# An attention stretch whose vector work follows the matmuls by hand, with z's norm on GpSimd

## The chip, the cores and the metric

The kernel runs on one core of a Trainium2 chip. A core has five engines with instruction streams of their own: TensorE (PE: matmuls and transposes into PSUM banks), VectorE (DVE), ScalarE (ACT), GpSimd (POOL) and SyncE (SP, which issues DMA transfers). Each executes its stream strictly in order, and an instruction that reads another engine's result waits on a semaphore; everything behind it on its engine waits too. The metric is the device time of one execution in microseconds; several executions are timed and the median is given.

## The reference, cut to what matters

One block of a streaming encoder on 512 tokens of width 1024, in f32: attention in two head groups, a gated feed-forward layer with a short convolution, and a gated embedding. The change touches the first group and the preparation of the second:

```python
h = rms_norm(x, attn_norm_g)
z = h @ W_in      # MLA q-latent 256 | kv-latent 128 | rope key 32 | diff q 512 | diff k 512 | diff v 512
# 8 MLA heads: q and k of 96 (64 + 32 with rope), v of 64, both normed per head
logits = q k^T * 96**-0.5;  masked;  probs = softmax(logits);  o = probs v
# 4 differential heads, each with two halves of 64:
q = rms_norm(dq.reshape(..., 4, 2, 64), q_g);  k = rms_norm(dk.reshape(..., 4, 2, 64), k_g)
logits = q k^T / 8 + bias[bucket(key - query)]
attn = softmax(first half) - lam * softmax(second half);  o = attn v
...
x += concat(o_mla, o_diff) @ W_out;  x += conv_ffn(x);  x += gated embedding
```

A query block of 128 sees only the keys up to its own block, since the mask is causal over chunks of 64.

## The kernel before, in words

All matmuls run in f32r; each operand is split into a high half (a cast on ScalarE, `hi`) and a low half (a subtraction on VectorE, `lo`), and a product is three matmuls (`mm3`, lines 157 to 159). Tokens lie in four blocks t = 0 to 3 of 128.

The MLA stretch (lines 771 to 832) is a loop over 16 steps i = 4 hp + t: pairs of heads hp = 0 to 3, query blocks t. A step makes, for the pair's two heads c:
- `mla_logits`: the logits of block t + 1 (TensorE), their negated maxima and the scaling of these (VectorE), and the exponentials with their sums (ScalarE);
- `mla_norm`: reciprocals of block t's sums and the scaling of its probabilities `pm` (VectorE);
- `mla_T`: transposes of block t's probabilities (TensorE, `pTm`) and copies of them to SBUF (`pt`, by VectorE or ScalarE in turn);
- `mla_pv`: the product with the values for the block before (TensorE, `mo`).
At t = 2 and t = 3 `mla_q` and `mla_k` transpose the next pair's queries and keys (`qT`, `kT`), and `split` makes their high and low halves `st`. Logits use three PSUM banks ("lg"), transposes two ("tp"): a transpose can start only when the tile before the last one has been read from its bank.

To keep TensorE busy between these, `pump(n)` inserts n *fill units* of the projection z = h W_in for the differential heads (`zd_units`): six matmuls each. The column blocks are c = 0 (queries), 1 (keys), 2 (values); c = 0 is done before the loop, c = 1 needs its units up to step 6, c = 2 the rest. `FILL_MLA = (1, 2, 2, 2)` is the number of units at t = 0 to 3. Weights of z come in four pieces per block (d0x, d1x, d2x), loaded by SP into three rotating raw buffers, then cast and subtracted.

`zd_out` scales a finished z block on ScalarE, squares it, and reduces the squares to `ssd` on VectorE. `zd_norm(c)` then makes the reciprocal roots `rd` of all 32 columns (4 blocks x 8 half-heads) by a Newton iteration on VectorE (`rms_v`), and scales the four blocks. `rms` is the other way to such a root that the kernel has: one VectorE operation and one GpSimd power (line 165).

`bias_strip` (step 3) builds the relative bias: GpSimd writes a row of 640 values, and issues three DMA transfers, each waiting for the one before (to memory, spread over 128 rows in memory, and back skewed), then a MEMSET on the tile that came back. Its row `vb` uses the buffer of an earlier z square.

What sets the order: TensorE's order is that of the code throughout. For VectorE, ScalarE and GpSimd a region with the same rule is open from the start of the kernel to step 2 (`region.__exit__`); after it a scheduler places their instructions, with a few held behind a named instruction (`tc.issue_after`), until a later region in the feed-forward part.

## Time and profile before

| | us |
|---|---|
| median of 3 runs | 652.36 (650.77 to 652.65) |
| profiled execution | 651.15 |
| its span, first to last instruction | 649.4 |
| TensorE busy in the span | 634.6 (98%) |
| VectorE, ScalarE, GpSimd busy | 489.2, 361.4, 57.5 |
| MLA stretch | about 66 to 165 of the span |

The granted clock of TensorE was 0.999 of full speed. Times in the rows below are microseconds from the span's start. A row of a timeline gives start, duration, engine, line and operation, output and inputs, shape, how many instructions are merged, and in brackets how long the engine was idle just before and which engine's instruction ended that. Buffer numbers are left out of the names: `st<-kT` stands for the split of any head's keys, `pTm` for any transposed probabilities.

### The profile page before, as it was taken

The numbers are of one execution on the slowest core, as the hardware profiler recorded it, in microseconds if no ns is written. First come the engines' busy times: TensorE is split into PE (matmuls) and PEld (weight loads), VectorE is DVE, ScalarE is ACT, GpSimd is POOL, SyncE is SP. The second block draws the span as 40 slices with busy tenths as digits, with TensorE's granted clock in tenths as the row PEclk, the third lists the DMA queues.
The fourth block names the chain that finished last, engine by engine and source line by source line (L and its number), as shares of the span: only waits on it lengthen the run. The fifth ranks groups of instructions, "written<-read, shape, count | busy, mean of one in ns | idle before, by whom it ended". The sixth has DMA issues, their size and how long they took to land.

```text
span 649.4 us, 10234 instructions
## 1 busy us (share of the span) xinstructions
PE 634.6 (98%) x3900; PEld 556.3 (86%) x3900; DVE 489.2 (75%) x898; ACT 361.4 (56%) x629; POOL 57.5 (9%) x92
## 2 busy tenths in 40 slices
PE   9999899899999999999999999999999999999997
PEld 9988677778788887889999999999999999988886
DVE  6889678668788776888886767676767677769844
ACT  7897557357567455656554645554554645547211
POOL 1510050000000121000100000000001100000000
PEclk9999999999999999999999999999999999999999
DMA  8351226033120337536675646465646463541121
GB/s 307 93 163 53 77 75 202 2 131 129 35 64 2 137 108 242 148 95 180 170 198 144 186 114 179 116 186 127 190 114 179 114 179 115 179 129 47 44 89 50
DMA packets 29913, 82.64 MB, mean 127 GB/s; under 512 B 3100, under 2 KB 4124, under 8 KB 29736
## 3 DMA queue, kind: packets, MB, share of 16 engines
q1 hardware_dynamic: 23816, 69.17, 32.0%
q0 software_dynamic: 5616, 12.33, 11.1%
q8 instruction: 31, 0.51, 0.3%
q10 hardware_dynamic: 432, 0.49, 0.2%
q14 instruction: 18, 0.15, 0.1%
HBM read 77.77 MB, written 5.52 MB: 128 GB/s over the span
## 4 chain that ended last, share of the span: by engine, by line
PE 84%; DVE 10%; ACT 4%; issue 1%; DMA 1%; ACTq 0%
PE dn L157 6%; PE dn L158 6%; PE dn L159 6%; PE gx L159 4%; PE gx L158 4%; PE gx L157 4%; PE g L157 3%; PE g L158 3%; PE g L159 3%; PE o L157 3%; PE o L159 2%; PE pg L159 2%; PE pg L158 2%; PE o L158 2%; PE pg L157 2%; PE zd L157 2%
## 5 line engine op out<-in xcount | busy, mean ns | idle before, releaser
L903 DVE TENSOR_TENSOR wSl<-rS,wSh 128x1024 fp32r<-128x1024 f32 x21 | 25.7, 1224 | 43.9 <-ACT wSh L899 43.7
L157 PE MATMUL dn<-ah,hi_dn 128*128 128x512 f32 x144 | 56.2, 391 | 0.0
L158 PE MATMUL dn<-al,hi_dn 128*128 128x512 f32 x144 | 56.2, 391 | 0.0
L159 PE MATMUL dn<-ah,lo_dn 128*128 128x512 f32 x144 | 56.0, 389 | 0.0
L1020 POOL DMA_DIRECT2D rS<-in_w_gu x19 | 22.7, 1195 | 250.6 <-DVE cv L1188 128.9
L899 ACT CAST wSh<-rS 128x1024 fp32r<-128x1024 f32 x21 | 22.1, 1052 | 36.1 <-PE gy L158 35.8
L157 PE MATMUL zd<-hi_d,xh 128*128 128x512 f32 x96 | 39.2, 409 | 0.0
L158 PE MATMUL zd<-lo_d,xh 128*128 128x512 f32 x96 | 37.8, 394 | 0.9 <-DVE lo_d L305 0.9
L669 DVE TENSOR_TENSOR x<-x,dn 128x512 f32<-128x512 f32 x44 | 29.9, 680 | 6.1 <-PE dn L159 6.1
L903 DVE TENSOR_TENSOR wTl<-rA,wTh 128x1024 fp32r<-128x1024 f32 x19 | 23.3, 1225 | 14.5 <-ACT wTh L899 14.0
L159 PEld LDWEIGHTS dn<-ah,lo_dn 128*128 128x128 f32 x144 | 27.0, 188 | 5.8
L157 PEld LDWEIGHTS dn<-ah,hi_dn 128*128 128x128 f32 x144 | 27.1, 188 | 5.1
L158 PEld LDWEIGHTS dn<-al,hi_dn 128*128 128x128 f32 x144 | 27.1, 188 | 5.0
L903 DVE TENSOR_TENSOR wAl<-rA,wAh 128x1024 fp32r<-128x1024 f32 x21 | 25.6, 1217 | 2.2 <-ACT wAh L899 2.2
L1191 ACT ACTIVATE cv<-cv 128x512 f32<-128x512 f32 x22 | 13.9, 631 | 23.9 <-DVE cv L1188 23.8
L899 ACT CAST wAh<-rA 128x1024 fp32r<-128x1024 f32 x21 | 22.1, 1053 | 8.9 <-DMA rA<-in_w_gu 8.6
L157 PE MATMUL g<-b2h,wAh 128*128 128x256 f32 (+1 forms) x88 | 26.4, 300 | 0.6 <-ACT g L1144 0.6
L157 PE MATMUL o<-yh,hi_o 128*128 128x512 f32 x64 | 26.9, 420 | 0.0
L718 ACT ACTIVATE pmd<-pmd,nmd 128x128 f32<-128x128 f32 (+3 forms) x32 | 17.9, 561 | 15.9 <-DVE nmd L717 15.9
L590 ACT ACTIVATE pm<-ml,sums,rq 128x128 f32<-128x128 f32 (+3 forms) x32 | 19.5, 616 | 12.6 <-DVE sums L583 7.5
L158 PE MATMUL g<-b2l,wAh 128*128 128x256 f32 (+1 forms) x88 | 26.3, 299 | 0.0
L159 PE MATMUL g<-b2h,wAl 128*128 128x256 f32 (+1 forms) x88 | 26.2, 297 | 0.0
(480 smaller groups left out, 2198.9 us busy)
## 6 DMA issues: line engine op xcount, KB each, us to landing
rA<-in_w_gu SPq DMA_DIRECT2D x22, 512.0 KB, 3.8
rS<-in_w_gu SPq DMA_DIRECT2D x22, 512.0 KB, 3.6
rS<-in_w_gu POOLq DMA_DIRECT2D x19, 512.0 KB, 6.0
raw_dn<-in_w_down SPq DMA_DIRECT2D x18, 512.0 KB, 5.9
raw_d<-in_w_d SPq DMA_DIRECT2D x12, 512.0 KB, 3.4
r<-in_w_gu SPq DMA_DIRECT2D x19, 256.0 KB, 5.8
raw_o<-in_w_out SPq DMA_DIRECT2D x8, 512.0 KB, 3.9
rS_pg<-in_w_pg SPq DMA_DIRECT2D x6, 512.0 KB, 4.0
```

The lines of the kernel that those rows point to most:

```text
L157: TE.matmul(ps, xh, wh, start=first and i == 0, stop=False, skip_group_check=again)
L158: TE.matmul(ps, xh, wl, start=False, stop=False, skip_group_check=again)
L159: TE.matmul(ps, xl, wh, start=False, stop=last and i == n - 1, skip_group_check=again)
L590: S.activation(pm[c], ps[c], AF.Exp, bias=nm[:, c:c + 1], scale=r[:, c:c + 1], accum_out=ssum[:, c:c + 1])
L669: V.tensor_tensor(xb(b), xb(b), ps, op=ALU.add)
L718: S.activation(pm[:, :n], pm[:, :n], AF.Exp, bias=nm, scale=-1.0, accum_out=s0 if m == 0 else s1)
L899: S.copy(h_, src)
L903: V.tensor_tensor(l_, src, _f32(h_), op=ALU.subtract)
L1020: nc.gpsimd.dma_start(sums[f].rearrange("p (i c) -> p i c", i=2), a["w_gu"][f][:, :2048].rearrange("p (i c) -> p i c", i=2)[:, :, :512], a ...
L1191: S.activation(cv, cv, AF.Silu)
```

## The change

The order of VectorE, ScalarE and GpSimd is that of the code through the whole MLA stretch: the region is closed in step 15 and not in step 2, and the `issue_after` holds in between are gone. The code is put in this order:
- `mla_norm` of a block comes ahead of the next block's logits (for t > 0), and the exponentials are a function of their own (`mla_exp`), at t = 2 one behind `mla_q` and one behind `mla_k`;
- `zd_norm` is split in two: `zd_root(c)` makes the roots by `rms`, so with a GpSimd power on 128x32, and `zd_scale(c, t)` scales one block. `rms_v` is no longer used for them;
- a table `extra` gives each step its share of the roots, of the scalings and of the casts and subtractions of the weights d2x; a second table, `late`, gives the first splits for the output product, behind the fill units of steps 13 and 14;
- `FILL_MLA` is (2, 1, 2, 2): one fill unit goes from t = 1 to t = 0.

```diff
-FILL_MLA = (1, 2, 2, 2)
+FILL_MLA = (2, 1, 2, 2)
...
-    def zd_norm(c):
-        rms_v(rd[:, c].rearrange("p t m -> p (t m)"), ssd[:, c].rearrange("p t m -> p (t m)"), 8 * NT, 64)
-        for t in range(NT):
-            zv = zd[c][t].rearrange("p (m d) -> p m d", d=64)
-            V.tensor_tensor(zv, zv, rd[:, c, t, :].unsqueeze(2).broadcast_to([P, 8, 64]), op=ALU.mult)
+    def zd_root(c):
+        rms(up(rd[:, c]), up(ssd[:, c]), 8 * NT, 64)
+
+    def zd_scale(c, t):
+        zv = zd[c][t].rearrange("p (m d) -> p m d", d=64)
+        V.tensor_tensor(zv, zv, rd[:, c, t, :].unsqueeze(2).broadcast_to([P, 8, 64]), op=ALU.mult)
...
-            S.activation(pm[c], ps[c], AF.Exp, bias=nm[:, c:c + 1], scale=r[:, c:c + 1], accum_out=ssum[:, c:c + 1])
         mla["pm", hp, t] = pm, pmf, sums, one
+
+    def mla_exp(hp, t, c):
+
+        ps, nm, r = mla["lg", hp, t]
+        pm, pmf, sums, one = mla["pm", hp, t]
+        S.activation(pm[c], ps[c], AF.Exp, bias=nm[:, c:c + 1], scale=r[:, c:c + 1], accum_out=sums[:, 1, c:c + 1])
...
+    extra = {
+        0: [lambda: lo(*z1_hi(3))],
+        3: [bias_strip],
+        4: [lambda: zd_root(0), lambda: z2_hi(0)],
+        5: [lambda: z2_lo(0)],
+        6: [lambda: zd_scale(0, 0), lambda: z2_hi(1)],
+        7: [lambda: zd_scale(0, 1), lambda: z2_lo(1), lambda: z2_hi(2)],
+        8: [lambda: z2_lo(2), lambda: z2_hi(3), lambda: zd_root(1), lambda: zd_scale(0, 2), lambda: zd_scale(0, 3)],
+        9: [lambda: z2_lo(3)],
+        10: [lambda: zd_scale(1, 0)],
+        11: [lambda: zd_scale(1, 1)],
+        12: [load_x, lambda: zd_scale(1, 2), lambda: zd_scale(1, 3)],
+    }
...
+            if t:
+                mla_norm(hp, t)
             if t < NT - 1:
                 mla_logits(hp, t + 1)
-            mla_norm(hp, t)
-            if i == 2:
-                region.__exit__(None, None, None)
-                held = tc.issue_after(mla["nm"].ins)
-                held.__enter__()
-            if i == 4:
-                held.__exit__(None, None, None)
-                with tc.issue_after(mla["k"].ins):
-                    zd_norm(0)
...
+                for c, (d, m) in enumerate(((diff_T, (0, 0)), (diff_T, (0, 1))) if last else ((mla_q, (2 * hp + 2,)), (mla_k, (2 * hp + 2,)))):
+                    d(*m)
+                    mla_exp(hp, t + 1, c)
...
+                    region.__exit__(None, None, None)
...
+            if t == 0:
+                mla_norm(hp, t)
+            for e in extra.get(i, ()):
+                e()
             pump(n)
```

Three places show what moved. First GpSimd, from the bias strip's transfers on (`vec1`, `vec2`: the rows in memory; `ro`: the roots of the differential heads' outputs, much later). Before:

```order
L637 DMA vec1_1052<-vb_1054 4x640
L638 DMA vec2_1053<-vec1_1052 128x2560
L641 DMA strip_1084<-vec2_1053 128x4x512
L642 MEMSET strip_1084 64x4x64
L746 TENSOR_TENSOR ro_2123<-mo_2122,mhalf_86 128x4
```

And now:

```order
L642 DMA vec1_1071<-vb_1073 4x640
L643 DMA vec2_1072<-vec1_1071 128x2560
L646 DMA strip_1103<-vec2_1072 128x4x512
L647 MEMSET strip_1103 64x4x64
L165 TENSOR_TENSOR rd_394<-rs_m_1161,mhalf_86 128x32
L165 TENSOR_TENSOR rd_394<-rs_m_1406,mhalf_86 128x32
L751 TENSOR_TENSOR ro_2101<-mo_2100,mhalf_86 128x4
```

The two powers for `rd` stand behind the strip's MEMSET.

Second VectorE in step 6 (pair 1, t = 2), around the splits of head 4's queries and keys (`qT4`, `kT4`), where `sums` are pair 1's last maxima, sums and reciprocals. Before:

```order
L151 TENSOR_TENSOR lo_d22_1279<-raw_d22_1276,hi_d22_1278 128x1024
L189 SCALAR_TENSOR_TENSOR st_123<-qT4_1282,qcol_117,st_123 96x512
L600 RECIPROCAL sums_1255<-sums_1255 128x1 x2
L151 TENSOR_TENSOR lo_d23_1341<-raw_d23_1338,hi_d23_1340 128x1024
L186 TENSOR_TENSOR st_123<-kT4_1289,st_123 96x512
L544 COPY pt_1322<-pTm120_1318 128x384
L397 TENSOR_REDUCE ssd_393<-sq_1304 128x8
L397 TENSOR_REDUCE ssd_393<-sq_1315 128x8
L601 TENSOR_SCALAR pm_1268<-pm_1268,sums_1255 128x512
```

And now:

```order
L189 SCALAR_TENSOR_TENSOR st_123<-qT4_1252,qcol_117,st_123 96x512
L186 TENSOR_TENSOR st_123<-kT4_1260,st_123 96x512
L405 TENSOR_TENSOR zd00_789<-zd00_789,rd_394 128x512
L398 TENSOR_REDUCE ssd_393<-sq_1282 128x8
L398 TENSOR_REDUCE ssd_393<-sq_1293 128x8
L543 COPY pt_1300<-pTm120_1296 128x384
L605 RECIPROCAL sums_1237<-sums_1237 128x1
L606 TENSOR_SCALAR pm_1250<-pm_1250,sums_1237 128x512
```

The subtractions of the weights d22 and d23 are gone from here, and the first scaling by `rd` stands ahead of the copy of `pTm120`.

Third VectorE at the turn from pair 1 to pair 2 (steps 7 and 8). Before:

```order
L403 TENSOR_TENSOR zd13_1313<-zd13_1313,rd_394 128x512
L544 COPY pt_1395<-pTm130_1390 128x512
L582 TENSOR_REDUCE sums_1410<-ml200_1411 128x2
L582 TENSOR_REDUCE sums_1423<-ml210_1424 128x2
L583 TENSOR_TENSOR sums_1410<-sums_1410,rq_505 128x2
L583 TENSOR_TENSOR sums_1423<-sums_1423,rq_505 128x2
L600 RECIPROCAL sums_1410<-sums_1410 128x2
```

And now:

```order
L405 TENSOR_TENSOR zd01_800<-zd01_800,rd_394 128x512
L305 TENSOR_TENSOR lo_d21_1272<-raw_d21_1269,hi_d21_1271 128x1024
L543 COPY pt_1356<-pTm130_1351 128x512
L581 TENSOR_REDUCE sums_1371<-ml200_1372 128x2
L582 TENSOR_TENSOR sums_1371<-sums_1371,rq_505 128x2
L581 TENSOR_REDUCE sums_1384<-ml210_1385 128x2
L582 TENSOR_TENSOR sums_1384<-sums_1384,rq_505 128x2
L605 RECIPROCAL sums_1371<-sums_1371 128x2
```

The scaled maximum that the first exponential waits for now follows its own reduction, and one scaling and one subtraction stand ahead where four scalings stood (the last of them, zd13, is shown).

## The prediction

> **What bounds the kernel now.** I read the page's first part, then TensorE's row of events through the MLA stretch (66 to 165 us), then for each gap the engine that ends it, and last the slow queues beside it.

> ```profile
> PE 634.6 (98%) x3900; PEld 556.3 (86%) x3900; DVE 489.2 (75%) x898; ACT 361.4 (56%) x629; POOL 57.5 (9%) x92
> ```

> TensorE is busy 634.6 of 649.4 us, and the change leaves its work as it is, so all that can be won is idle time, 14.8 us in the whole program. The stretch that the change touches holds these gaps (TensorE's timeline: start, duration, then in brackets the idle time and who ended it):

> ```profile
> 72.90 0.50 PE L158 MATMUL zd<-lo_d,xh 128*128 128x512 f32 x1 [0.85 <-DVE lo_d L305]
> ...
> 79.41 0.63 PE L539 MATMUL pTm<-ident,pm 128*128 128x128 f32 x4 [0.78 <-DVE pm L601]
> ...
> 91.17 1.25 PE L539 MATMUL pTm<-ident,pm 128*128 128x128 f32 x8 [0.25 <-DVE st L189]
> ...
> 98.29 0.43 PE L539 MATMUL pTm<-ident,pm 128*128 128x128 f32 x2 [2.09 <-DVE pm L601]
> ...
> 110.78 0.55 PE L539 MATMUL pTm<-ident,pm 128*128 128x128 f32 x3 [0.69 <-DVE st L186]
> ...
> 122.45 0.43 PE L539 MATMUL pTm<-ident,pm 128*128 128x128 f32 x2 [1.72 <-DVE pm L601]
> ...
> 144.48 0.44 PE L539 MATMUL pTm<-ident,pm 128*128 128x128 f32 x2 [0.26 <-DVE pm L601]
> ...
> 163.33 0.65 PE L699 MATMUL d1T<-ident,zd 128*128 128x128 f32 x4 [0.21 <-ACT pt L542]
> 164.46 1.09 PE L620 MATMUL mo<-pt,kvb 128*64 128x128 f32 x16 [0.47 <-DVE pt L544]
> ```

> They sum to 7.32 us: 4.66 up to 111 us, 1.98 in the next two rows, 0.68 at the end. Nearly all wait for VectorE; its own backlog (scalings of z, low halves of weights) stands ahead of what TensorE needs. 7.3 us is the most that the change can bring.

> **Part 1: the removed reciprocal roots.** The Newton iteration of `zd_norm` is 12 small VectorE operations, twice. Its first and last:

> ```profile
> 91.63 0.17 DVE L170 TENSOR_SCALAR rs_n<-ssd 128x32 f32<-128x32 f32 x1
> ...
> 94.09 0.19 DVE L175 SCALAR_TENSOR_TENSOR rd<-rs_t,rd 128x32 f32<-128x32 f32 x1
> ```

> From 91.63 to 94.28 is 2.65 us, less a copy of about 0.6 that runs between: 2 us each time, 4 in all. VectorE is idle a quarter of the span, so this is no gain by itself; it helps where VectorE is late.

> **Part 2: the power that replaces them, and its queue.** `zd_root` issues one VectorE operation (0.17) and one GpSimd power on 128x32. The trace has the power only on narrower tiles; beside it stand GpSimd's chain for the bias strip and a plain addition of the same width:

> ```profile
> 23.47 1.04 POOL L165 TENSOR_TENSOR rx<-rs_m,mhalf 128x4 f32<-128x4 f32 x1 [4.62 <-DVE rs_m L164]
> ...
> 29.48 0.25 POOL L384 TENSOR_TENSOR kr<-kr,krt 128x32 f32<-128x32 f32 x1
> 30.74 1.65 POOL L165 TENSOR_TENSOR rl<-rs_m,mhalf 128x8 f32<-128x8 f32 x1 [1.00 <-DVE rs_m L164]
> ...
> 81.65 7.55 POOL L636 TENSOR_SCALAR vb<-tab 4x207 f32<-4x207 f32 x27 [46.32 <-DVE ssd L397]
> 89.53 0.78 POOL L637 DMA_DIRECT2D vec<-vb  x1 [0.32 <-POOL vb L636]
> 91.89 0.60 POOL L638 DMA_DIRECT2D vec<-vec  x1 [1.59 <-DMA vec<-vb]
> 99.97 0.81 POOL L641 DMA_DIRECT2D strip<-vec  x1 [7.47 <-PE mo L620]
> 108.15 0.31 POOL L642 MEMSET strip<- 64x256 f32 x1 [7.38 <-DMA strip<-vec]
> ```

> Four more columns cost 0.61 us, 0.152 each; 24 more than eight make 1.65 + 3.66 = 5.3 us. Bounds: not below the 1.65 of the narrower tile, not above four times it, 6.6. I take 5.3, since both rows lie on one line.

> [...]

> The power for z's query block (c=0) stands in GpSimd's queue behind the strip's MEMSET, which waits for three transfers in a row. In the kernel before nothing needed for the next steps stood behind it. VectorE's input to it (`rs_m`) is long there. The chain's head waits for the reduction `ssd` of the first z block, which waits for ScalarE's square:

> ```profile
> 80.88 0.69 DVE L397 TENSOR_REDUCE ssd<-sq 128x8 f32<-128x512 f32 x1 [1.35 <-ACT sq L396]
> ```

> In the new order the same logits, exponentials and square stand ahead of it, so I leave the chain where it is: MEMSET ends at 108.46, the roots are ready at R = 108.46 + 5.31 = 113.8 us.

> **Part 3: the wait this adds.** `zd_scale(0, 0)` stands on VectorE in step 6 (pair 1, t=2), right behind the low half of head 4's keys. In the trace before that place is reached at 110.7, with three weight subtractions (1.2 us each) ahead of it that now come later:

> ```profile
> 108.92 1.20 DVE L151 TENSOR_TENSOR lo_d<-raw_d,hi_d 128x1024 fp32r<-128x1024 f32 x1
> 110.04 0.68 DVE L186 TENSOR_TENSOR st<-kT,st 96x512 fp32r<-96x512 f32 x1
> 110.64 0.54 DVE L544 COPY pt<-pTm 128x384 f32<-128x384 f32 x1
> 111.11 1.26 DVE L397 TENSOR_REDUCE ssd<-sq 128x8 f32<-128x512 f32 x2
> 112.29 0.87 DVE L601 TENSOR_SCALAR pm<-pm,sums 128x512 f32<-128x512 f32 x2
> ...
> 116.60 2.50 DVE L403 TENSOR_TENSOR zd<-zd,rd 128x512 f32<-128x512 f32 x4
> ```

> So VectorE stands there some 3 to 7 us. Queued behind: two reductions, the copy of the transposed probabilities pT120, pair 1's last normalisation. TensorE waits for the copy: head 5's query transpose needs that copy's PSUM bank ("tp" has two). From R on: one scaling 0.61 (four take 2.50, of which the last is 0.68), two reductions 1.18 (111.11 to 112.29), copy 0.54, hand-over 0.07: the transpose starts at R + 2.4 = 116.2. Before:

> ```profile
> 113.34 0.60 PE L551 MATMUL qT<-ident,qn 128*96 128x128 f32 x4
> ...
> 117.69 0.33 PE L157 MATMUL ml<-st 100*128 100x128 f32 x1
> ...
> 124.98 0.39 PE L157 MATMUL zd<-hi_d,xh 128*128 128x512 f32 x1
> ...
> 127.72 0.60 PE L539 MATMUL pTm<-ident,pm 128*128 128x128 f32 x4
> ```

> With the 4.66 us of early gaps gone, TensorE could be there at 108.7: it stands 7.5 us. The early gain is swallowed whole and 2.8 us more are lost. This holds however much of the 4.66 really goes, since R doesn't depend on it.

> **Part 4: what is won behind it.** From that transpose to pair 2's first logits took 4.35 us; I keep it (120.5). Next late is VectorE, with a scaling, a weight subtraction and the copy pT130 (0.6 + 1.15 + 0.6) ahead of pair 2's first maximum: st<-kT5, at 115.56 before, ends about 119, so the maximum starts near 121.3. The maximum was at 119.62 before, the normalisation at 122.02, done at 122.5:

> ```profile
> 115.56 0.68 DVE L186 TENSOR_TENSOR st<-kT,st 96x512 fp32r<-96x512 f32 x1
> ...
> 119.62 1.01 DVE L582 TENSOR_REDUCE sums<-ml 128x2 f32<-128x256 f32 x2
> ...
> 122.02 0.48 DVE L601 TENSOR_SCALAR pm<-pm,sums 128x128 f32<-128x128 f32 x2
> ```

> The same 2.9 us give 124.2. One of TensorE's fill units moves ahead of t=0's transposes (two units take 2.74, from 124.98 to 127.72), so these come at 120.5 + 1.5 + 2.74 = 124.7. No wait: the 1.72 goes, and the 0.26 of pair 3 likewise. At t=1, where the unit is taken away, the normalisation now stands ahead of the next logits' maxima, and one unit covers it. The 0.68 at the end I leave: the copies that end those gaps now have two weight subtractions in front instead of one.

> The second power (5.3) starts near 124.5, and z's scaling that needs it stands behind head 6's split in step 10, nine or more us on: hidden. If it took twice as long it would stall as the first does. Casts and subtractions of the four d2 weights move off steps 4 to 6 into 4 to 9; each is ahead of its matmuls by a unit or more.

> **Sum:** -4.66 + 7.5 - 1.98 = +0.8 us. On the profiled execution (651.15) that is 652.0; on the median of the runs (652.36) 653.2. The four times shown average 651.7, and I predict 652.5.

> **Rivals.**
> 1. *The power is cheap at 128x32.* For: the flat addition (0.25 at 32 columns). Against: 0.61 us for four columns. At 1.65, R = 110.1 and the transpose starts at 112.5, 0.8 earlier than before; with 1.98 behind it -2.8: 648.9.
> 2. *No wait at all*: the chain ends before VectorE needs the roots. All of 6.64 goes: 645.1. For: little here. Against: MEMSET at 108.15 already lies where VectorE arrives.
> 3. *Slower: the strip lands later.* The last d2 load was issued just ahead of the strip's transfer:

> ```profile
> 99.54 0.33 SPq L142 DMA_DIRECT2D raw_d<-in_w_d  x1
> 103.18 7.34 SPq L142 DMA_DIRECT2D raw_o<-in_w_out  x3
> ...
> 100.00:102.00 2.00, 2.00 (x12) 1.79 (x11) 1.96 (x8) 0.72 (x2) 0.77 (x1) 1.00 0.71 229
> ```

> Its buffer is now freed by a subtraction near 101, so its 512 KB would move beside the strip's 1024 KB: at 229 GB/s (last column) up to 2.3 us more, R = 116.1, 654.8. Against: the three raw_o loads, which ran beside the strip from 103 on, now come after 119. It decides from a MEMSET later than 109.3, 1.2 us behind where it is now, where the sum passes 2 us.

> **How the numbers follow.** Forecast 0.60, rival 1 0.14, rival 2 0.06, rival 3 0.20. About 0.3% (2 us) is what a measurement here tells from no change. Faster: both fast rivals and a little of the forecast, 0.23; slower: most of rival 3 and a little of the forecast, 0.20; same 0.57. The power's bounds alone (1.65 to 6.6) span 648.9 to 653.8; with the strip a us either way and rival 3 the range is 648.3 to 655.0.

> **What would show it.** Right: on GpSimd a power on 128x32 of about 5.3 us right behind the MEMSET; on VectorE the first zd scaling waiting for GpSimd until about 114; on TensorE one gap of 5 us or more at a query transpose that waits for a pt copy, and no gap at 122 or later but the last two. Wrong: a power under 3 us, a MEMSET before 106, or new gaps at other transposes, where ScalarE's or VectorE's fixed order holds something back that I haven't priced.

## The result: 4.4 us faster, outside the predicted range

| | before | changed |
|---|---|---|
| median of 6 runs each | 652.13 us (650.47 to 653.05) | 647.73 us (646.98 to 649.42) |
| profiled execution, its span | 651.15, 649.4 | 647.4, 645.4 |

The ratio of changed to before is 0.994, with a 95% interval of 0.992 to 0.9959. I had predicted 652.5 us, 648.3 to 655.0, most likely no change. The change is faster, and more than the range allowed.

First the page's first part of the changed kernel, to be held against the same row of before:

```profile
PE 633.0 (98%) x3900; PEld 555.6 (86%) x3900; DVE 486.7 (75%) x878; ACT 360.6 (56%) x629; POOL 67.3 (10%) x94
```

VectorE has 20 instructions fewer; GpSimd is busy 9.8 us more, with two powers of 11.9 us in sum. Now the gaps in TensorE's timeline over the same stretch (start, duration, idle time before and who ended it):

```profile
67.03 0.64 PE L550 MATMUL qT<-ident,qn 128*96 128x128 f32 x4 [0.47 <-DVE st L189]
...
76.73 0.50 PE L158 MATMUL zd<-lo_d,xh 128*128 128x512 f32 x1 [0.23 <-DVE lo_d L305]
...
81.62 0.64 PE L557 MATMUL kT<-ident,kvb 128*96 128x128 f32 x4 [0.63 <-ACT pt L541]
...
85.29 1.19 PE L538 MATMUL pTm<-ident,pm 128*128 128x128 f32 x6 [0.28 <-DVE st L189]
...
110.36 0.64 PE L550 MATMUL qT<-ident,qn 128*96 128x128 f32 x4 [0.60 <-ACT pt L541]
112.52 0.64 PE L557 MATMUL kT<-ident,kvb 128*96 128x128 f32 x4 [1.52 <-DVE pt L543]
...
116.35 0.33 PE L157 MATMUL ml<-st 100*128 100x128 f32 x1
...
160.22 0.65 PE L704 MATMUL d1T<-ident,zd 128*128 128x128 f32 x4 [1.15 <-ACT pt L541]
```

None waits any more for a normalised block (`pm`), which was the cause of the two largest gaps before (2.09, 1.72) and of the 0.78. The wait that I had forecast is there, at the right place in time, and small: 0.60 and 1.52 us around 110 to 112.5 and not 7.5. Pair 2's first logits start at 116.35; before it was 117.69, and I had predicted 120.5. By the transposes of `d1T` TensorE is at 160.22 and was at 163.33, so 3.1 of the 4.0 us by which the span is shorter are won inside the stretch, and its last wait of before (0.47 at the product behind them) is gone too. The gaps went from 7.32 to 4.88 us in sum, 2.4 less; the rest of the 4.0 is in stretches that TensorE's timeline shows as busy (634.6 to 633.0), and I can't split it further.

Why the wait stayed small stands in GpSimd's timeline of the changed kernel, from the bias strip on:

```profile
81.90 6.63 POOL L641 TENSOR_SCALAR vb<-tab 4x207 f32<-4x207 f32 x27 [46.45 <-DVE sums L605]
...
99.00 0.80 POOL L646 DMA_DIRECT2D strip<-vec  x1 [7.18 <-DMA vec<-vec]
104.34 0.30 POOL L647 MEMSET strip<- 64x256 f32 x1 [4.54 <-DMA strip<-vec]
104.62 5.47 POOL L165 TENSOR_TENSOR rd<-rs_m,mhalf 128x32 f32<-128x32 f32 x1
121.00 6.41 POOL L165 TENSOR_TENSOR rd<-rs_m,mhalf 128x32 f32<-128x32 f32 x1 [10.91 <-DVE rs_m L164]
```

The power takes 5.47 us, as I had worked out (5.3). But the MEMSET that it stands behind starts at 104.34, where it started at 108.15 before: the strip's transfer, issued at 99.00, landed within 5.3 us and not 8.1. So the roots are ready at 110.1 and not at 113.8, and VectorE waits for them 3.70 us; had they come at 113.8, the same wait would have been 7.4:

```profile
105.74 0.69 DVE L186 TENSOR_TENSOR st<-kT,st 96x512 fp32r<-96x512 f32 x1 [0.41 <-ACT st L185]
110.12 0.69 DVE L405 TENSOR_TENSOR zd<-zd,rd 128x512 f32<-128x512 f32 x1 [3.70 <-POOL rd L165]
110.73 1.27 DVE L398 TENSOR_REDUCE ssd<-sq 128x8 f32<-128x512 f32 x2
111.92 0.55 DVE L543 COPY pt<-pTm 128x384 f32<-128x384 f32 x1
```

The two open questions after the result: what made the transfer faster, and what, if not the powers and not the whole order, brought the gain.

### The profile page after: what moved, and what is told of

It reads as the page before. It is cut to its first block, busy times and chain, and to the rows that moved or that the text cites. A ratio compares the mean times of both kernels' runs of the same rounds, so it can differ in the third digit from the quotient of the medians.

```text
span 645.4 us, 10213 instructions
## 1 busy us (share of the span) xinstructions
PE 633.0 (98%) x3900; PEld 555.6 (86%) x3900; DVE 486.7 (75%) x878; ACT 360.6 (56%) x629; POOL 67.3 (10%) x94
## 4 chain that ended last, share of the span: by engine, by line
PE 78%; DVE 9%; ACT 5%; DMA 4%; POOL 2%; issue 2%; ACTq 0%; DVEq 0%; POOLq 0%
PE dn L158 6%; PE dn L157 6%; PE dn L159 6%; PE gx L159 4%; PE gx L158 4%; PE gx L157 4%; PE g L157 3%; PE g L158 3%; PE g L159 3%; PE o L157 3%; PE o L159 2%; PE o L158 2%; PE pg L157 2%; PE pg L158 2%; PE pg L159 2%
## 5 line engine op out<-in xcount | busy, mean ns | idle before, releaser
L157 PE MATMUL dn<-ah,hi_dn 128*128 128x512 f32 x144 | 56.2, 391 | 0.0
L158 PE MATMUL dn<-al,hi_dn 128*128 128x512 f32 x144 | 56.2, 391 | 0.0
L157 PE MATMUL zd<-hi_d,xh 128*128 128x512 f32 x96 | 39.3, 410 | 0.0
L158 PE MATMUL zd<-lo_d,xh 128*128 128x512 f32 x96 | 37.7, 392 | 0.2 <-DVE lo_d L305 0.2
L157 PEld LDWEIGHTS dn<-ah,hi_dn 128*128 128x128 f32 x144 | 27.1, 188 | 5.2
L158 PEld LDWEIGHTS dn<-al,hi_dn 128*128 128x128 f32 x144 | 27.1, 188 | 4.9
L157 PE MATMUL g<-b2h,wAh 128*128 128x256 f32 (+1 forms) x88 | 26.4, 300 | 0.5 <-ACT g L1164 0.5
L157 PE MATMUL o<-yh,hi_o 128*128 128x512 f32 x64 | 26.9, 420 | 0.0
L158 PE MATMUL g<-b2l,wAh 128*128 128x256 f32 (+1 forms) x88 | 26.2, 297 | 0.0
L1431 ACT ACTIVATE sg<-sg 128x512 f32<-128x512 f32 (+1 forms) x9 | 5.3, 584 | 36.8 <-DVE sg L1430 36.8
```

The costliest lines, as they stand in the source:

```text
L157: TE.matmul(ps, xh, wh, start=first and i == 0, stop=False, skip_group_check=again)
L158: TE.matmul(ps, xh, wl, start=False, stop=False, skip_group_check=again)
L1431: S.activation(sg, sg, AF.Sigmoid)
```

## The experiments

Nine kernels with an edit ran, then the changed kernel and one of the nine once more (e10_after_again, e11_fill_back_again). Ratios are against the kernel before, timed beside the run, with the 95% interval; those of the changed kernel are 0.994 (0.992 to 0.9959), and 0.9909 (0.9886 to 0.9932) when it ran again.

### 1. The Newton roots back, all else as changed (e1_newton)

```diff
     def zd_root(c):
-        rms(up(rd[:, c]), up(ssd[:, c]), 8 * NT, 64)
+        rms_v(up(rd[:, c]), up(ssd[:, c]), 8 * NT, 64)
```

> The changed kernel, but both roots of z's norm are made on VectorE again (12 small operations, 2.65 us each time by the trace of before), at the places where the changed kernel issues them; nothing waits for GpSimd. Theory A (what is left of the loss is the wait for the power behind the strip's MEMSET, 0.60 + 1.52 us of TensorE's gaps at head 5's transposes): those two gaps go, about 2.1 us less than the changed kernel, some 645.6 us. Rival B (VectorE is the limit there, and the time that the power took off it was the gain): the added 2.65 us on VectorE at steps 4 and 8 open gaps at the transposes of steps 5 and 9, and the time stays at 647.7 or rises by up to 2 us.

646.57 us, ratio 0.9924 (0.9906 to 0.9942). The wait at head 5's key transpose fell from 1.52 to 0.18, the 0.60 before it stayed:

```profile
110.40 0.64 PE L550 MATMUL qT<-ident,qn 128*96 128x128 f32 x4 [0.60 <-ACT pt L541]
111.22 0.64 PE L557 MATMUL kT<-ident,kvb 128*96 128x128 f32 x4 [0.18 <-DVE pt L543]
```

So the power costs 1.3 us of waiting at this place; the 0.60 isn't its doing (ScalarE ends it). Part of that comes back elsewhere: with Newton roots a gap of 0.37 opens at a transpose at t = 1 (123.68, behind `pm`), which the changed kernel doesn't have, and the spans differ by 0.4 us (645.0 and 645.4). The median is 1.2 us lower, but the intervals of the ratios overlap, and that of the second run of the changed kernel (0.9909) lies lower still. The power in this place is no gain; that it is a loss of the whole kernel isn't shown.

### 2. The first power ahead of the strip's chain (e2_root_first)

```diff
+        2: [lambda: zd_root(0)],
         3: [bias_strip],
-        4: [lambda: zd_root(0), lambda: z2_hi(0)],
+        4: [lambda: z2_hi(0)],
```

> The changed kernel with one move: the first root (one VectorE operation and the GpSimd power) is issued in step 2, ahead of the bias strip's chain on GpSimd, and not in step 4 behind it. The power then runs at about 85 us, the strip's chain starts behind it, some 8 us later, and the strip is needed only near 155 us. Theory A: VectorE's wait at the first scaling (3.70 us in the changed kernel) goes, TensorE's two gaps of 0.60 and 1.52 us at head 5's transposes with it, about 645.6 us. Rival B (other vector work stands in the way as soon as the wait is gone): gaps of the same size appear at the next transposes, and the time stays at 647.7 within 0.7 us.

645.57 us, ratio 0.9908 (0.9889 to 0.9926). GpSimd's timeline:

```profile
85.32 5.46 POOL L165 TENSOR_TENSOR rd<-rs_m,mhalf 128x32 f32<-128x32 f32 x1 [50.11 <-DVE rs_m L164]
...
113.62 0.30 POOL L647 MEMSET strip<- 64x256 f32 x1 [4.68 <-DMA strip<-vec]
```

The same power, 19 us earlier, waits for nothing; the strip comes 9.3 us later, and nothing has to wait for that. The key transpose's gap is 0.17; the 0.60 before it stays, against my first theory. That the price of the power at this transpose is its place behind the MEMSET is thereby shown. This run and experiment 1 were timed together: with the power in the free place the median is 1.0 us below that with Newton roots (645.57 and 646.57), so there the power is worth something.

### 3. The casts and subtractions of d2 packed into fewer steps (e3_early_loads)

```diff
-        4: [lambda: zd_root(0), lambda: z2_hi(0)],
-        5: [lambda: z2_lo(0)],
-        6: [lambda: zd_scale(0, 0), lambda: z2_hi(1)],
-        7: [lambda: zd_scale(0, 1), lambda: z2_lo(1), lambda: z2_hi(2)],
-        8: [lambda: z2_lo(2), lambda: z2_hi(3), lambda: zd_root(1), lambda: zd_scale(0, 2), lambda: zd_scale(0, 3)],
+        4: [lambda: zd_root(0), lambda: z2_hi(0), lambda: z2_lo(0)],
+        5: [lambda: z2_hi(1), lambda: z2_lo(1)],
+        6: [lambda: z2_hi(2), lambda: z2_lo(2), lambda: zd_scale(0, 0)],
+        7: [lambda: zd_scale(0, 1)],
+        8: [lambda: z2_hi(3), lambda: zd_root(1), lambda: zd_scale(0, 2), lambda: zd_scale(0, 3)],
```

> The changed kernel with the casts and subtractions of the weights d2 packed into steps 4 to 6 as they lay in the kernel before, so that the raw buffers come free early and the loads raw_d23, raw_o00 and raw_o01 fall just ahead of the strip's transfer and beside it again. Theory L (those loads made the strip land in 8.1 us and not 5.3): the strip takes about 8 us, its MEMSET starts near 107.5 and not 104.3, the power ends near 113, TensorE's gaps at head 5's transposes grow from 2.1 to about 5 us, and the time is about 650.5 us. Rival M (the strip's 8.1 us had another cause, such as VectorE's traffic or one slow execution): the strip still lands in 5 to 6 us, and the time stays near 647.7 us.

650.0 us, ratio 0.9966 (0.9949 to 0.9983). The strip took 7.8 us again (the issues of transfers, with us from issue to landing last), and the key transpose waited 2.35, behind 0.66 at the query transpose (together 3.0; I had expected 5):

```profile
strip<-vec POOLq DMA_DIRECT2D x1, 1024.0 KB, 7.8
```

```profile
114.36 0.64 PE L557 MATMUL kT<-ident,kvb 128*96 128x128 f32 x4 [2.35 <-DVE pt L543]
```

So with the loads the strip's time comes back. But this edit moved both the last d2 load ahead of the strip and the output loads beside it, and it packs VectorE's work (gaps of 0.69 and 0.43 open ahead of these transposes); the next one moves one load.

### 4. One load ahead of the strip (e8_one_load)

```diff
-        4: [lambda: zd_root(0), lambda: z2_hi(0)],
-        5: [lambda: z2_lo(0)],
+        4: [lambda: zd_root(0), lambda: z2_hi(0), lambda: z2_lo(0)],
```

> The changed kernel with the subtraction of weight d20 one step earlier (step 4), so that its raw buffer comes free earlier and the load of the last d2 weight (512 KB) is issued ahead of the strip's transfer and not behind it; the loads for the output product stay where they are. Theory A (a 512 KB load issued just ahead is what slows the strip): the strip lands in 7 to 8.2 us, the MEMSET starts at 106 to 107, the first power ends at about 112, VectorE waits for it 5.5 us or so, TensorE's gap at head 5's key transpose grows from 1.52 to 2.5 to 3.5 us, time 648.5 to 650. Theory B (the loads for the output product, which run beside the strip in the kernel before, are what slows it, and here they still come after it): 5.2 to 5.5 us, MEMSET at 104.3, the gap stays 1.5, time 647.5 to 648.

651.65 us, ratio 0.9985 (0.9971 to 0.9999). One subtraction a step earlier frees a raw buffer, and with it the last d2 load is issued at 99.69, 0.6 us ahead of the strip; in the changed kernel it was issued at 101.96, 3.0 us behind it. SP's queue, the strip's issue and MEMSET, and the power, of e8_one_load:

```profile
99.69 0.33 SPq L142 DMA_DIRECT2D raw_d<-in_w_d  x1
...
100.31 0.79 POOL L646 DMA_DIRECT2D strip<-vec  x1 [7.54 <-PE ml L159]
107.84 0.30 POOL L647 MEMSET strip<- 64x256 f32 x1 [6.73 <-DMA strip<-vec]
108.11 5.46 POOL L165 TENSOR_TENSOR rd<-rs_m,mhalf 128x32 f32<-128x32 f32 x1
```

and SP's queue of the changed kernel, whose strip was issued at 99.00:

```profile
101.96 0.33 SPq L142 DMA_DIRECT2D raw_d<-in_w_d  x1
```

The strip landed in 7.5 us with no output load near (the first came at 120.24). So it is the 512 KB load just ahead that slows it, as the first theory said. The kernel before has the same pair: load at 99.54, strip at 99.97. What the DMA queues moved differs too (GpSimd's queue is q0, which carries the strip, SP's is q1; packets, MB, share of the 16 engines' time). The changed kernel from 102 to 104 us, then e8_one_load from 104 to 106:

```profile
q0 software_dynamic: 189, 0.71, 86.7%
q1 hardware_dynamic: 30, 0.12, 14.9%
```

```profile
q0 software_dynamic: 123, 0.45, 60.4%
```

In the changed kernel the strip moves 0.71 MB in its two us, and the load issued behind it hardly moves until the strip is through (0.12 MB; from 104 on it moves alone). In e8_one_load no other queue moves a byte from 104 to 106, so the load ahead is through, and still the strip moves only 0.45 MB. So the cause is not that two transfers share a rate while both move; why a strip behind a load stays slow isn't settled here.

The price was higher than I expected of this run (648.5 to 650). The roots were ready at 113.57, and TensorE waited 4.05 us; behind that wait its granted clock (third column from the end) fell to half, and the matmuls of the next unit took 0.63 us and not 0.39:

```profile
111.32 0.64 PE L550 MATMUL qT<-ident,qn 128*96 128x128 f32 x4 [0.60 <-ACT pt L541]
116.01 1.09 PE L557 MATMUL kT<-ident,kvb 128*96 128x128 f32 x4 [4.05 <-DVE pt L543]
...
117.33 0.63 PE L158 MATMUL zd<-lo_d,xh 128*128 128x512 f32 x1
```

```profile
116.00:118.00 2.00, 1.99 (x7) 1.77 (x8) 1.93 (x6) 0.86 (x2) 0.00 (x0) 0.50 0.03 8
118.00:120.00 2.00, 2.00 (x7) 1.51 (x7) 2.00 (x3) 0.66 (x1) 0.00 (x0) 0.50 0.00 0
```

From that transpose to pair 2's first logits TensorE took 6.46 us (116.01 to 122.47) and in the changed kernel 3.83 (112.52 to 116.35), so 2.6 us of slow clock come on top of 2.5 us of longer wait. The stretch also began 1.0 us later in this execution (the row `zd<-lo_d` at 77.69, there at 76.73); together that is 6.1, near the 6.0 by which the span is longer (651.4 against 645.4). The profiled execution was the slowest of ten (653.28).

### 5. The fill unit alone, on the kernel before (e5_fill_only)

```diff
-FILL_MLA = (1, 2, 2, 2)
+FILL_MLA = (2, 1, 2, 2)
```

> The kernel before with the fill units (2, 1, 2, 2) and nothing else of the change. Theory F (the extra unit covers the softmax at t = 0): the gaps of 2.09, 1.72 and 0.26 us at the transposes of t = 0 shrink by up to 1.37 us each, 3.0 us together, less what opens at t = 1, so 649.5 to 651. Rival O (VectorE's backlog under the scheduler's order is what holds, and only moves to the next transposes): no change, 652.5 within 1 us.

648.4 us, ratio 0.9932 (0.9911 to 0.9953): as good as the whole change, and better than I had expected of it. TensorE's gaps at t = 0, which were 2.09, 1.72 and 0.26:

```profile
98.10 0.44 PE L539 MATMUL pTm<-ident,pm 128*128 128x128 f32 x2 [0.73 <-DVE pm L601]
...
120.89 0.43 PE L539 MATMUL pTm<-ident,pm 128*128 128x128 f32 x2 [0.36 <-DVE pm L601]
...
160.32 0.66 PE L699 MATMUL d1T<-ident,zd 128*128 128x128 f32 x4 [0.21 <-ACT pt L542]
```

The third is gone, and 0.19 opens at t = 2 of the last pair (153.09). `d1T` is reached at 160.32, against 160.22 in the changed kernel. One number in a table does what the fixed order, the table `extra`, the powers and that number do together.

### 6. The change without its fill unit, twice (e4_fill_back, e11_fill_back_again)

```diff
-FILL_MLA = (2, 1, 2, 2)
+FILL_MLA = (1, 2, 2, 2)
```

> The changed kernel with the fill units as before, (1, 2, 2, 2): one unit of 1.37 us goes back from t = 0 to t = 1. Theory F (the fill unit covers the softmax at t = 0): gaps come back at the transposes of t = 0, some 0.5 to 1.4 us in each of four pairs, the time rises by 2 to 4 us, to 650 or 651. Rival O (the order of VectorE removed those gaps by itself): the gaps at t = 0 are under 0.3 us each, and the time stays within 0.7 us of 647.7.

648.93 us, ratio 0.9949 (0.993 to 0.9968). The gaps at t = 0 don't come back; the rest of the change holds each at 0.26 or 0.27:

```profile
95.62 0.44 PE L538 MATMUL pTm<-ident,pm 128*128 128x128 f32 x2 [0.26 <-DVE pm L606]
...
112.53 1.04 PE L557 MATMUL kT<-ident,kvb 128*96 128x128 f32 x4 [1.38 <-DVE pt L543]
...
121.06 0.43 PE L538 MATMUL pTm<-ident,pm 128*128 128x128 f32 x2 [0.26 <-DVE pm L606]
```

So the fill unit and the rest of the change are two remedies for the same gaps: each takes most of them, and together they win little more than either. Of the rest I take the order to be what does it; no run has the order without the power and without the fill unit. The profiled execution was slower than its gaps explain, since the clock fell behind the 1.38 us wait (a window and its length, then the busy times of TensorE, its weight loads, VectorE, ScalarE and GpSimd; third column from the end: the granted clock):

```profile
109.22:112.63 3.41, 1.44 (x9) 0.72 (x8) 2.46 (x6) 1.85 (x4) 0.88 (x1) 1.00 0.00 0
112.63:116.05 3.42, 3.42 (x11) 2.71 (x12) 3.38 (x7) 1.53 (x2) 0.00 (x0) 0.50 0.02 5
```

The changed kernel's own profile has 1.00 there after a wait of 1.52. Whether that belongs to the program or to the execution I asked by running both again without an edit.

> The changed kernel with FILL_MLA as before, (1, 2, 2, 2), once more, nothing else edited. In its first profile TensorE waited 0.60 and 1.38 us at head 5's transposes and its clock then was 0.50 for two us, span 647.6. Theory D (of the program): the same again, clock 0.66 and 0.50 in the four us behind the second wait, span 647 to 648. Theory W (of the execution): it may stay at 1.00, and then the span is 645.5 to 646, as the gaps alone would make it.

> The changed kernel once more, nothing edited, to see whether TensorE's granted clock behind its two short waits at head 5's transposes (0.60 and 1.52 us in the first profile, clock 1.00) is a property of the program or of the execution. Theory D (of the program): the clock stays at 1.00 from 110 to 120, span 645 to 646. Theory W (of the execution): it may fall to 0.5 there in this profile, and then the span is about 2 us longer, 647 to 648, with the same two gaps.

Both again: e11_fill_back_again waited 0.60 and 1.25 us and the clock stayed at 1.00; e10_after_again waited even longer and it stayed too:

```profile
112.66 0.64 PE L557 MATMUL kT<-ident,kvb 128*96 128x128 f32 x4 [2.56 <-DVE pt L543]
```

```profile
107.58:110.99 3.41, 1.92 (x10) 1.11 (x8) 0.73 (x2) 2.43 (x5) 2.64 (x1) 1.00 0.00 0
110.99:114.40 3.41, 1.74 (x10) 1.43 (x10) 3.34 (x9) 1.06 (x2) 0.00 (x0) 1.00 0.02 5
```

So one program loses clock in one execution and not in the next, and the length of the wait alone doesn't decide it. What does, as far as these traces show it, stands in the last section. The spans were 645.2 (e10_after_again) and 646.8 (e11_fill_back_again), a us more than I expected of the latter; at `d1T` they are level (160.40 and 160.57), so that microsecond lies behind the stretch, and its cause is open.

### 7. The power alone, on the kernel before (e6_power_only)

```diff
     def zd_norm(c):
-        rms_v(rd[:, c].rearrange("p t m -> p (t m)"), ssd[:, c].rearrange("p t m -> p (t m)"), 8 * NT, 64)
+        rms(rd[:, c].rearrange("p t m -> p (t m)"), ssd[:, c].rearrange("p t m -> p (t m)"), 8 * NT, 64)
```

> The kernel before with the GpSimd power in place of the Newton iteration in zd_norm and nothing else of the change. The scheduler then places the first two scalings of z right behind the copy pT030 near 94 us. Theory A (VectorE waits in its order for the power behind the strip's MEMSET): VectorE stands from about 94 until the MEMSET (104.3 to 108.2) and a power of 5.5 us, 110 to 114, TensorE waits at the transposes of pair 1's t = 0 some 13 to 17 us, 664 to 669 us. Rival N (the power is ready when it is needed): 651 to 653 us.

667.72 us in one run. Here all four scalings stand close behind the roots on VectorE, and TensorE waits out both powers:

```profile
104.84 0.66 PE L539 MATMUL pTm<-ident,pm 128*128 128x128 f32 x2 [6.94 <-DVE pm L601]
```

The second time it is 6.26 us, and around the two waits the clock stood at 0.50 for 6.8 and 10.2 us. My expectation had the power behind the MEMSET; the scheduler put it ahead of the strip's issue (94.22). The gap of this size is thus the whole power and not its queue, and that the time fell into the range that I had expected (664 to 669) is luck: I had one long wait, and there were two and a slow clock.

### 8. The change with the scheduler (e7_scheduler)

```diff
+            if i == 2:
+                region.__exit__(None, None, None)
...
-                    region.__exit__(None, None, None)
```

> The changed kernel with the region of fixed order closed in step 2, as in the kernel before; code order, fill units, split roots and the GpSimd power stay. The scheduler then moves the first root ahead of the bias strip, near 72 us, with the scalings of z right behind it. Theory S (the fixed order is needed because the scheduler doesn't place the scalings by the power's 5.5 us): VectorE waits about 5 us near 72, TensorE some 4 us at the first transposes, and without the later wait (2.1 us) the time is about 649.5 to 652 us. Rival T (the order of the code and the fill units are the gain, the fixed order adds nothing): 645.6 to 647.7 us.

660.63 us, ratio 1.012 (1.0095 to 1.0145), slower than before. The scheduler moves the power ahead (70.39) and the first scaling right behind it, so VectorE and then TensorE wait for the whole of it:

```profile
77.23 0.47 PE L158 MATMUL ml<-st 100*128 100x128 f32 x1 [5.09 <-DVE st L186]
...
127.23 1.97 PE L538 MATMUL pTm<-ident,pm 128*128 128x128 f32 x8 [5.26 <-DVE st L189]
```

The expectation had the direction right; the loss is larger than it said (649.5 to 652), since the second power is waited out as well, and the clock stood at 0.50 for 6.8 and 10.2 us around the two waits. With the power, the fixed order is needed: it keeps the scalings away from it. With Newton roots and the fill unit it wins little that these runs can tell (0.9924 with it in experiment 1, 0.9932 without it in experiment 5).

### 9. A version that beats both (e9_best)

From what 1, 2 and the profile showed: the first power in step 2; the cast of weight d21 from step 6 to step 5 (it delayed ScalarE's copy, hence the 0.60); and two output weights cast only behind ScalarE's last copy of the stretch, `cp` (hence the 1.15 at `d1T`).

```diff
+        2: [lambda: zd_root(0)],
         3: [bias_strip],
-        4: [lambda: zd_root(0), lambda: z2_hi(0)],
-        5: [lambda: z2_lo(0)],
-        6: [lambda: zd_scale(0, 0), lambda: z2_hi(1)],
+        4: [lambda: z2_hi(0)],
+        5: [lambda: z2_lo(0), lambda: z2_hi(1)],
+        6: [lambda: zd_scale(0, 0)],
...
-            w = wo_w(kq, dq)
+            if kq == 0 and dq in (1, 2):
+                with tc.issue_after(cp):
+                    w = wo_w(kq, dq)
+            else:
+                w = wo_w(kq, dq)
```

> The changed kernel with the first root in step 2, ahead of the bias strip; the cast of d21 in step 5 and not 6; and the weights o01 and o02 of the output product held behind the last copy of MLA probabilities on ScalarE. Against the run with the first root in step 2 alone (645.6 us) the gaps left there are 0.60 and 0.17 us at head 5's transposes, behind ScalarE's cast of d21 and the squares, and 1.16 us at the first key transpose of the differential heads, behind ScalarE's casts of the output weights. Theory A: both go, 643.7 to 644.3 us. Rival B (the next instruction of the same engine takes their place): 645.6 within 0.7 us.

644.1 us, ratio 0.9866 (0.9845 to 0.9886). What is left of the gaps, with 0.20 and 0.16 besides:

```profile
82.05 0.64 PE L557 MATMUL kT<-ident,kvb 128*96 128x128 f32 x4 [0.61 <-ACT pt L541]
...
157.31 0.66 PE L708 MATMUL d1T<-ident,zd 128*128 128x128 f32 x4 [0.21 <-ACT pt L541]
```

## Why the prediction was wrong, step by step

**What bounds the kernel: right for the gaps, not complete.** Of their sum of 7.32 us the change took 2.4, e9_best 6.1 (1.2 left). But 1.6 of the 4.0 us by which the span is shorter lie in TensorE's busy time, which the prediction held fixed, and in the medians e9_best wins 9.0 us (653.1 to 644.1), more than the 7.3 that I called the most. And behind waits the clock stood at 0.50 for 3.41 to 10.24 us in five of the traces (experiments 3, 4, 6, 7 and 8), which the sum of the gaps doesn't contain; in the profiled execution of before it held (last section).

**Part 1, the removed Newton roots: right.** Taking them off VectorE brings nothing by itself; with them put back the kernel is not slower (experiment 1). Where the power has no queue in front, it is 1.0 us better than they are (experiment 2).

**Part 2, the power's size: right**, 5.47 for 5.3. The two narrow powers (1.04 us at 4 columns, 1.65 at 8) lie nearly on one line with the wide one. Rival 1's cheap power (1.65 at 32 columns) is out.

**Part 2, "I leave the chain where it is": the step that failed.** It put the MEMSET's end at 108.46; it came at 104.64, 3.8 us sooner, 2.8 of them by the strip's transfer and the rest by its earlier issue, most of that by a shorter `vb` (6.63 us, before 7.55). The step argued over logits, exponentials and the square ahead of the chain, and these did come at nearly the same time (`vb` starts at 81.90, before 81.65). It didn't ask what set the strip's 8.1 us. That was the d2 load issued 0.43 us ahead of it, and the change moved that load behind the strip (experiment 4). I had quoted both rows, and used them in rival 3 for the opposite: there the moved load was to slow the strip from behind, and the output loads, which leave, were the argument against. Neither decides: with a load issued 3.0 us behind, the strip landed in 5.3 us (the changed kernel), and without an output load near it was slow all the same, 7.5 us (experiment 4).

How much hung on this step experiment 4 shows: it puts the load back, the roots are ready at 113.57 (my R was 113.8), and the kernel takes 651.65 us (I had predicted 652.5). With the premise true the sum comes out near, though not term by term, and so partly by luck: the wait is then 0.60 + 4.05 us and not 7.5, and 2.6 us of slow clock, for which I had no term, make up most of the difference.

**Part 3, the wait: right mechanism, wrong transpose.** From R on I counted a scaling, two reductions, the copy and the hand-over, 2.4 us; TensorE went on 2.4 us after R in the changed kernel (110.1 to 112.52) and in experiment 4 (113.57 to 116.01). But it is head 5's key transpose that needs this copy's bank, not its query transpose: the latter needs the copy that ScalarE makes. So TensorE does 0.6 us of work more before it stands. And the early gain isn't swallowed whole: I had TensorE at the query transpose at 108.7; it was there at 109.76, since 1.61 us of the early gaps were left or new (0.47, 0.23, 0.63, 0.28). With R at 110.1 the wait comes to 0.60 + 1.52 = 2.1 us, not 7.5. In my sum this one term is 5.4 us too large. Since TensorE goes on 2.4 us after R in any case, the 3.7 us by which R came sooner are most of the 4.1 by which pair 2's first logits came sooner than forecast (116.35 and 120.5). With what was measured the sum is -3.05 (early gaps, 4.66 to 1.61) + 2.12 - 1.98 + 0.47 (the end, below) = -2.4, the change of the gaps, and not +0.8.

**Part 4, what is won behind it: right in kind.** The 1.72 and the 0.26 went, and none opened at t = 1. By the sum that was 1.98. What I missed is that the unit moved at t = 0 also takes 1.36 of the 2.09 in the early part, so that it alone wins as much as the whole change (experiment 5); I had credited those 4.66 to the order without asking which edit took them, and then cancelled them against the wait. At the end 0.68 was to stay; it grew to 1.15, because casts of output weights stand ahead of ScalarE's copy there, not because of VectorE's subtractions as I had it. The second power was hidden, as forecast, though it took 6.41 us.

**The rivals.** In time the result (647.73) is nearest to rival 1 (648.9, chance 0.14), and by luck: its roots at R = 110.1 and its transpose at 112.5 are what was measured (110.1 and 112.52), but from a power of 5.47 us behind an early MEMSET, where rival 1 had one of 1.65 behind a late one. In mechanism it lies on the way to rival 2 (no wait, 645.1, chance 0.06), whose condition is that the chain ends before VectorE needs the roots: the chain ended sooner, though not soon enough. I dismissed rival 2 with the MEMSET's place in the kernel before, the same step again. Rival 3 named the right thing, the strip's transfer and the d2 load beside it, with the wrong sign.

**What would show it wrong** named a MEMSET before 106. It was that.

## What to carry to other kernels

Where a prediction rests on a transfer's landing time in the old trace, look at what is issued just ahead of it on every queue, and whether the change moves that too; a time that was measured beside a load is not the transfer's own (here 7.5 to 8.2 us with a load issued just ahead, 5.2 to 5.5 in most of the runs without). Try each edit of a mixed change alone before crediting any: here two of them remove the same gaps, and a third, the one that looks like the saving, is no gain where it stands. A slow operation moved to an idle engine belongs where its queue is empty, with its users some steps off (here 645.57 us in experiment 2, against 647.73 behind the strip's chain), and it needs an order that keeps them there (660.63 without, experiment 8).

## What the runs showed of the hardware

**A transfer's neighbour.** The strip's 1024 KB on GpSimd's queue landed in 5.2 to 5.5 us in the kernels where no 512 KB load was issued within the microsecond before it (the changed kernel, 1, 2, 6, 7, 8), and in 7.5 to 8.2 us in the four where one was (before, 3, 4, 5). One case is outside both, 6.9 us in e9_best, where the load was 7 us ahead. There the strip wasn't slow: its queue had moved the data by 114.4, 4.9 us after the issue, as in the changed kernel (by 103.97, 5.0 us). Only the landing came late, for a reason that the trace doesn't show.

```profile
94.62:98.03 3.41, 1.58 (x8) 0.98 (x6) 3.41 (x10) 1.93 (x6) 0.00 (x0) 1.00 0.87 234
```

```profile
110.78:114.19 3.41, 2.16 (x14) 1.54 (x12) 3.34 (x9) 1.80 (x3) 0.00 (x0) 1.00 0.02 5
```

Ahead of each fall inside a program stands a piece with less work: 1.44 us of 3.41 in e4_fill_back, 1.06 in experiment 3, 0.12 in 4, at most 0.65 in 7 and 8. So in all 13 traces the clock falls after a piece with at most 1.44 us of work (the piece ahead of the last fall included) and holds after one with at least 1.58, by the trace's busy times. By this, the two executions of one program differ in where the pieces lie: in e4_fill_back the waits of 0.60 and 1.38 us are in one piece, in e11_fill_back_again those of 0.60 and 1.25 are in two. The wait of 2.56 in e10_after_again lies across two pieces as well. Why the clock goes by such pieces these traces don't show.

It reaches the medians. The kernel before was timed 44 times beside the experiments: the 32 executions with a mean granted clock of 0.994 to 0.997 have a median of 653.0 us, the 12 with 0.998 or more (the profiled one, at 0.999, among them) 651.0. One piece at 0.50 costs up to 1.7 us, half of 3.41, and lowers the mean clock by 0.003 (an estimate from these figures), which fits. The kernels whose single waits are all under 1.2 us (e1_newton, e2_root_first, e5_fill_only, e9_best) had 0.998 or more in every execution. So a part of what a closed gap is worth, about 2 us here, isn't in the profile of an execution in which the clock held. That it is the waits of this stretch that cost the others their clock isn't shown, since they left no profile.

**A power beside VectorE.** On 128x32 it took 5.45 to 5.47 us where VectorE was idle or up to two thirds busy, 5.81 where it was busy for 4.72 us of them (experiment 3), and 6.41 to 6.44 where it was busy nearly throughout. But the second power of the changed kernel took 6.41 us in one execution and 5.82 in the next, with VectorE as busy both times. The first power of experiment 2, then the second of the changed kernel and of e10_after_again (third busy time: VectorE's):

```profile
85.32:90.78 5.46, 5.46 (x37) 4.31 (x38) 3.61 (x8) 2.67 (x5) 5.46 (x2) 1.00 0.00 2
```

```profile
121.00:127.41 6.41, 6.41 (x48) 5.26 (x48) 6.20 (x17) 2.76 (x7) 6.41 (x1) 1.00 0.35 105
```

```profile
121.13:126.95 5.82, 5.82 (x42) 4.72 (x43) 5.64 (x16) 2.77 (x7) 5.82 (x1) 1.00 0.29 97
```

VectorE was busy 3.61 of 5.46 us, 6.20 of 6.41 and 5.64 of 5.82. So the powers beside a VectorE that was busy for most of the time are the longer ones, 5.81 to 6.44 us against 5.45 to 5.47. The busy share alone doesn't give the size, no run here varied VectorE's load alone, and why they are longer isn't shown.
